# Feed-through matrices of a state space layer in four column groups of the array, their triangular form copied in sixteen pieces a chunk

## The chip, the cores and the metric

The kernel runs on one core of a Trainium2 chip. The metric is the device time of one execution in microseconds (us): the median of the runs is 2045.85 us (three runs, 2044.94 to 2045.88). Engines are named as the profile names them: PE (matrix products, its weight loads apart as PEld), DVE (vector), ACT (scalar), POOL and SP (DMA queue).

## The reference, cut to what matters

Two blocks run one after the other on 256 tokens of width 1024, all in float32: an attention and mixture-of-experts block, then a block with a retention layer, a gated feed-forward layer (ffn 0), a state space layer ("s5") and a second feed-forward layer (ffn 1). The change touches the set-up of the s5 layer alone. Of it the reference computes, for 64 groups of 16 inputs with 64 complex states each:

```python
mag = jnp.exp(lr * dt); ar = mag * jnp.cos(li * dt); ai = mag * jnp.sin(li * dt)
...
bbr = fr[..., None] * br - fi[..., None] * bi          # input matrix, real part; bbi likewise
...
_, _, s_r, s_i = lax.associative_scan(combine, (a_r, a_i, bu_r, bu_i), axis=0)
y = einsum('lbgp,gip->blgi', s_r, c_re) - einsum('lbgp,gip->blgi', s_i, c_im)
y = y.reshape(bsz, L, D_MODEL) + d_skip * u
```

The kernel doesn't scan over all 256 tokens. It takes four tokens as one step. Inside a step, output token n depends on input token m of the same step, for m no later than n, through a small matrix C A^(n-m) B, and for n = m through the skip weights `d_skip` too. Those matrices hold only weights, so they can be made at any time before the layer runs.

## The kernel before, in words

The 64 groups are worked off in eight chunks of eight groups. A chunk is four pairs q = 0 to 3, each of two groups, which is 32 inputs and 128 states. `s5_parts` makes one chunk's matrices and puts them into a scratch tensor in memory; the s5 layer loads them later. `second_block` calls it through `prepare`, at a priority lowered by LOW = 300, in the retention layer and the first 20 steps of ffn 0. The scheduler that builds the program then fits its instructions in between those of the layers: in the trace the products of the eight chunks run between 1405 and 1645 us, in the last product of the retention layer and in ffn 0. Each engine works through one fixed list in order, so an instruction that waits holds everything behind it.

For one chunk, `s5_parts` does this. POOL clears the buffers `R`, `o` and `T` (L1414 to L1416; each exists once, so it waits for the chunk before). DVE works out B times powers of A and C times powers of A (L1394, L1408). ACT copies them into `R` and `CA` (L1430, L1438, L1439). PE transposes `R` (L1443), ACT copies that (L1444), and a DMA on SP's queue stores it (L1445). Then the part that is changed: PE multiplies B with C A^n for the four pairs (L1449, eight products of 32 x 128 results, contraction over 128 states, real and imaginary part accumulated). All four pairs write to the same 32 rows of the bank, side by side. ACT copies the result to `K` (L1452, 32 partitions x 512). DVE adds the skip weights on the diagonal of token distance 0 (L1394 for `dd` and for `K`). ACT copies `K` four times into the block-triangular matrix `T`, block row st holding `K` shifted by 32 st columns (L1457, four copies of 32 partitions x 512, 384, 256 and 128). A DMA on SP's queue stores `T` (L1458). The priority is raised again (`high_priority`) for the copies and products.

Around it, the layers multiply streamed weights in three products each: every half panel of 128 x 1024 weights is split by ACT into a rounded part (L147) and by DVE into the rest (L148), and PE then makes 24 products with it (L251 to L253, 24 a half panel, 256 columns each). Splits run ahead of the products as far as buffers allow (`AHEAD` = 2, four buffers). ACT and DVE also do the activation of ffn 0 (L1602 to L1610).

Elsewhere the kernel already writes to column groups: `ada_tile` (L405), early in the program, multiplies 32 columns of weights into four of them, rows 32c to 32c+32 of one bank, 512 columns each.

Of the kernel before, what the change touches and what calls it, by code (L numbers as in the profile page):

```python
# [8 lines left out]
F32 = mybir.dt.float32  # L9
# [4 lines left out]
ALU = mybir.AluOpType  # L14
# [40 lines left out]
def bc(ap, dim, n):  # L55

    a = list(ap.ap)
    a.insert(dim, [0, n])
    return bass.AP(tensor=ap.tensor, offset=ap.offset, ap=a)
# [1317 lines left out]
def s5_parts(tc, g, c, tp, ps):  # L1377


    nc, A = tc.nc, g.A  # L1380
    v, s, pe = nc.vector, nc.scalar, nc.tensor
    q0 = 4 * c
    o = tp.tile([128, 2304], F32, tag="s5o", name="s5o")
    T = tp.tile([128, 4, 128], F32, tag="s5T", name="s5T")
    RT = o[:, 0:1024].rearrange("p (q i m) -> p q i m", q=4, i=2)
    CA = [o[:, 1024 + 640 * i:1664 + 640 * i].rearrange("p (q n) -> p q n", q=4) for i in range(2)]
    bcin = tp.tile([128, 4, 4, 16], F32, tag="s5b", name="s5b")
    nc.sync.dma_start(out=bcin, in_=A["s5_bc"][c])
    br, bi, cr, ci = (bcin[:, j] for j in range(4))
    fr, fi = (bc(g.fc[:, j, q0:q0 + 4], 2, 16) for j in range(2))  # L1390
    t = tp.tile([128, 4, 4, 16], F32, tag="s5t", name="s5t")

    def tt(o_, a, b, op):
        v.tensor_tensor(out=o_, in0=a, in1=b, op=op)  # L1394

    def powers(u, i0, n, x0, x1, ap, neg):

        ar, ai = (bc(ap[:, :, j, q0:q0 + 4], 3, 16) for j in range(2))
        y0, y1 = bc(x0, 1, n), bc(x1, 1, n)
        u0, u1 = (u[:, j, i0:i0 + n] for j in range(2))  # L1400
        tt(u0, ar, y0, ALU.mult)
        tt(t[:, :n], ai, y1, ALU.mult)
        tt(u0, u0, t[:, :n], ALU.subtract)
        tt(u1, ar, y1, ALU.mult)
        tt(t[:, :n], ai, y0, ALU.mult)
        if neg:
            u1, tn = (x.rearrange("p n q f -> p (n q f)") for x in (u1, t[:, :n]))
            v.scalar_tensor_tensor(out=u1, in0=u1, scalar=-1.0, in1=tn, op0=ALU.mult, op1=ALU.subtract)  # L1408
        else:
            tt(u1, u1, t[:, :n], ALU.add)  # L1410


    R = tp.tile([128, 2, 4, 4, 2, 16], F32, tag="s5R", name="s5R")
    nc.gpsimd.memset(R, 0.0)  # L1414
    nc.gpsimd.memset(o[:, 1024:2304], 0.0)
    nc.gpsimd.memset(T, 0.0)  # L1416
    u = tp.tile([128, 2, 4, 4, 16], F32, tag="s5u", name="s5u")
    b0, b1 = u[:, 0, 3], u[:, 1, 3]
    tt(b0, br, fr, ALU.mult)
    tt(t[:, 0], bi, fi, ALU.mult)  # L1420
    tt(b0, b0, t[:, 0], ALU.subtract)
    tt(b1, bi, fr, ALU.mult)
    tt(t[:, 0], br, fi, ALU.mult)
    tt(b1, b1, t[:, 0], ALU.add)
    powers(u, 0, 3, b0, b1, g.apr, False)
    with tc.high_priority():
        for j in range(2):
            for h in range(2):
                r = slice(64 * h, 64 * h + 64)
                s.copy(out=R[r, j, :, :, h].rearrange("p q s f -> p s q f"), in_=u[r, j])  # L1430
    u = tp.tile([128, 2, 4, 4, 16], F32, tag="s5u", name="s5u")
    powers(u, 0, 4, cr, ci, g.ap[:, 1:], True)
    with tc.high_priority():
        for j in range(2):
            for h in range(2):
                r = slice(64 * h, 64 * h + 64)
                ca = CA[j].rearrange("p q (n h f) -> p n q h f", n=5, h=2)[r, :, :, h]
                s.activation(out=ca[:, 0], in_=bcin[r, 2 + j], func=ACTF.Copy, scale=1.0 - 2.0 * j)  # L1438
                s.copy(out=ca[:, 1:], in_=u[r, j])  # L1439
        for j in range(2):  # L1440
            b = ps()
            for q in range(4):
                pe.transpose(out=b[:, q * 128:(q + 1) * 128], in_=R[:, j, q].rearrange("p s h f -> p (s h f)"), identity=g.ident)  # L1443
            s.copy(out=RT[:, :, j], in_=b.rearrange("p (q m) -> p q m", q=4))  # L1444
        nc.sync.dma_start(out=g.s5dram[c][:, :2304], in_=o)  # L1445
        b = ps()
        for q in range(4):
            for j in range(2):
                pe.matmul(out=b[:32, q * 128:(q + 1) * 128], lhsT=R[:, j, q, 3].rearrange("p h f -> p (h f)"), rhs=CA[j][:, q, :128],  # L1449
                          start=(j == 0), stop=(j == 1))  # L1450
        K = tp.tile([32, 4, 4, 32], F32, tag="s5K", name="s5K")
        s.copy(out=K, in_=b[:32].rearrange("p (q n m) -> p q n m", q=4, n=4))  # L1452
        dd = tp.tile([32, 4, 32], F32, tag="s5d", name="s5d")
        tt(dd, bc(g.ident[:32, :32], 1, 4), bc(g.s5d[:, q0:q0 + 4], 2, 32), ALU.mult)
        tt(K[:, :, 0], K[:, :, 0], dd, ALU.add)
        for st in range(4):
            s.copy(out=T[32 * st:32 * st + 32, :, 32 * st:128], in_=K[:, :, :4 - st].rearrange("p q n m -> p q (n m)"))  # L1457
        nc.sync.dma_start(out=g.s5dram[c][:, 2304:], in_=T.rearrange("p q n -> p (q n)"))  # L1458


def second_block(tc, g, out):
# [33 lines left out]
    def prepare(n=1):  # L1495

        for i in range(prepared[0], min(prepared[0] + n, 10)):
            with tc.high_priority(offset=-LOW):
                if i < 2:
                    s5_powers(tc, g, i, s5p)  # L1500
                else:
                    s5_parts(tc, g, i - 2, s5p, later_bank)
        prepared[0] += n
# [444 lines left out]
def tile_body(ctx, tc, A, out):  # L1948
    nc = tc.nc
    g = Ctx()  # L1950
    g.A, g.nc = A, nc
    cst = ctx.enter_context(tc.tile_pool(name="cst", bufs=1))
    wst = ctx.enter_context(tc.tile_pool(name="wstage", bufs=NSTAGE))
    wsp = ctx.enter_context(tc.tile_pool(name="wsplit", bufs=AHEAD + 2))
    st = Stream(nc, wst, NSTAGE, 2048)
# [72 lines left out]
    nc.vector.tensor_scalar(out=e, in0=e, scalar1=1.0, scalar2=None, op0=ALU.add)  # L2028
    nc.vector.reciprocal(out=e, in_=e)
    nc.vector.tensor_tensor(out=g.c2, in0=g.pv("c_2"), in1=e, op=ALU.mult)  # L2030
    g.s5d = cst.tile([32, 32], F32, name="s5d")
    nc.scalar.dma_start(out=g.s5d, in_=A["s5_d"])
    g.cst = cst
    g.ada = Columns(g, g.c2, mod2, g.pv("ada_b"), [ADA_ORDER.index(i) for i in (1, 4, 7, 10)])
# [16 lines left out]
def host_arrays(inputs):  # L2051
    import numpy as np

    def cat(*a):
        return np.ascontiguousarray(np.concatenate(a, axis=0))

    def colblocks(w, nb, kper):

        K, N = w.shape
        t = w.reshape(K // (128 * kper), kper, 128, N // nb, nb).transpose(3, 0, 2, 1, 4)  # L2060
        return t.reshape(-1, 128, kper * nb)
# [4 lines left out]
    I = {k: np.asarray(a) for k, a in inputs.items()}  # L2066
    d = {}
# [31 lines left out]
    bs = [I[f"s5_{n}_2"][0].reshape(8, 4, 2, 64, 16).transpose(0, 2, 3, 1, 4).reshape(8, 128, 4, 16) for n in ("b_re", "b_im")]  # L2099
    cs = [I[f"s5_{n}_2"][0].reshape(8, 4, 2, 16, 64).transpose(0, 2, 4, 1, 3).reshape(8, 128, 4, 16) for n in ("c_re", "c_im")]  # L2100
    d["s5_bc"] = np.stack(bs + cs, axis=2)
    d["s5_d"] = I["s5_d_2"][0].reshape(32, 32).T
    d["ada_w"] = cat(*(colblocks(I["ada_w_2"][i // 6][:, i % 6 * 1024:(i % 6 + 1) * 1024], *((512, 4) if i in ADA_PE else (1024, 2)))
                       for i in ADA_ORDER))

    def blocks(w, order):

        K, N = w.shape
        t = w.reshape(K // 128, 128, N // 128, 128).transpose(2, 0, 1, 3)[order]
# [14 lines left out]
    f = np.float32  # L2124
# [9 lines left out]
    c, s = np.cos(ang).astype(f), np.sin(ang).astype(f)  # L2134
# [28 lines left out]
```

## Time and profile before

| | |
|---|---|
| median of three runs | 2045.85 us |
| profiled execution | 2045.55 us |
| its span (first to last instruction) | 2043.9 us |
| mean granted clock of PE | 0.98 |
| PE busy | 1943.4 us, 95% |
| DVE busy | 1104.8 us, 54% |
| ACT busy | 649.2 us, 32% |

Shares over the whole span mix stages. From about 300 to 1200 us the expert layer streams weights; there DVE and ACT have little to do. In the retention layer and ffn 0 DVE is busy 80 to 95% and ACT 50 to 70% of the time. The difference between the profiled execution and its span, 1.65 us, lies before the first and behind the last instruction.

### The profile page before, as it was taken

The page shows a single profiled execution, that of the slowest core. Times are in us where ns is not written, and L with a number is a line of the kernel's source. Part 1 is how long each engine was busy: PE and PEld are TensorE (multiplying, and loading weights), DVE is VectorE, ACT ScalarE, POOL GpSimd, SP SyncE. Part 2 cuts the span into 40 slices and gives each one's busy share as a digit, 9 for nine tenths or more (in the row PEclk, how much of TensorE's full clock was granted, in tenths as well). Part 3 has the DMA queues.
Part 4 walks back from the last instruction along what each step waited for, and adds up shares of the span by engine and source line. Part 5 has one row for each costly group of instructions (what it writes and reads, how often), then busy time and mean ns, then how long its engine had stood idle before and what let it go on. Part 6 is the DMA issues. An engine that isn't in the chain of part 4 may idle for free. (4 is left out here: it accounts for less than half of the span.)

```text
span 2043.9 us, 29004 instructions
## 1 busy us (share of the span) xinstructions
PE 1943.4 (95%) x11188; PEld 1256.4 (61%) x11188; DVE 1104.8 (54%) x2360; ACT 649.2 (32%) x1134; POOL 59.0 (3%) x92
## 2 busy tenths in 40 slices
PE   6999989999999999999989999999999999999998
PEld 4756844333233333343333338888999998699998
DVE  3856654322222122132212238998898879779863
ACT  5455211000000000010000014445677645256542
POOL 1000010000000000000000000000011002100000
PEclk9999989999999999999999998999999999799999
DMA  8657659999999999999989994767677877555651
GB/s 342 223 197 282 240 193 413 427 426 427 426 427 427 426 427 427 426 421 387 427 366 427 426 394 159 259 235 267 228 258 260 288 279 295 206 193 195 226 178 63
DMA packets 101758, 643.41 MB, mean 315 GB/s; under 512 B 11584, under 2 KB 12880, under 8 KB 34288
## 3 DMA queue, kind: packets, MB, share of 16 engines
q1 hardware_dynamic: 94176, 613.46, 75.8%
q0 software_dynamic: 6624, 26.76, 3.8%
q8 instruction: 89, 1.46, 0.3%
q10 hardware_dynamic: 816, 1.30, 0.2%
q14 instruction: 53, 0.43, 0.1%
HBM read 626.79 MB, written 14.68 MB: 314 GB/s over the span
## 5 line engine op out<-in xcount | busy, mean ns | idle before, releaser
L956 PE MATMUL hc<-w,xe 128*64 128x512 f32 (+1 forms) x2008 | 470.3, 596 | 29.5 <-DMA w<-in_w_in_dram 28.3
L956 PEld LDWEIGHTS hc<-w,xe 128*64 128x64 f32 (+1 forms) x2008 | 145.4, 138 | 338.7 <-issue 244.0
L148 DVE TENSOR_TENSOR parts<-w,parts 128x1024 fp32r<-128x1024 f32 x238 | 289.8, 1222 | 64.2 <-ACT parts L147 60.0
L147 ACT CAST parts<-w 128x1024 fp32r<-128x1024 f32 x238 | 248.6, 1047 | 200.3 <-PE b L253 116.5
L251 PE MATMUL b<-h2h,parts 128*128 128x256 f32 x896 | 255.9, 286 | 1.4 <-ACT h2h L1527 0.9
L252 PE MATMUL b<-h2l,parts 128*128 128x256 f32 x896 | 255.5, 285 | 1.3 <-DVE h2l L1528 0.9
L956 PE MATMUL yb<-w,hb 128*64 128x512 f32 (+1 forms) x1024 | 252.5, 603 | 2.1 <-SPq L1205 1.6
L253 PE MATMUL b<-h2h,parts 128*128 128x256 f32 x896 | 254.3, 284 | 0.0
L976 DVE COPY hs<-hc 128x512 f32<-128x512 f32 x33 | 22.8, 691 | 405.3 <-PE hc L956 405.3
L251 PEld LDWEIGHTS b<-h2h,parts 128*128 128x128 f32 x896 | 170.1, 190 | 4.0 <-ACT h2h L1527 3.0
L252 PEld LDWEIGHTS b<-h2l,parts 128*128 128x128 f32 x896 | 169.9, 190 | 3.7 <-DVE h2l L1528 2.1
L253 PEld LDWEIGHTS b<-h2h,parts 128*128 128x128 f32 x896 | 169.8, 190 | 0.6 <-issue 0.6
L974 ACT COPY hs<-hc 128x512 f32<-128x512 f32 x33 | 19.3, 585 | 429.9 <-PE hc L956 429.9
L956 PEld LDWEIGHTS yb<-w,hb 128*64 128x64 f32 (+1 forms) x1024 | 68.1, 138 | 132.1 <-issue 120.9
L203 DVE SCALAR_TENSOR_TENSOR acc<-w,c,acc 128x1024 f32<-128x1024 f32 x77 | 98.5, 1279 | 7.3 <-DMA w<-in_ada_w_dram 7.0
L251 PE MATMUL b<-ah,parts 128*128 128x256 f32 x352 | 101.3, 288 | 0.7 <-ACT parts L147 0.6
L253 PE MATMUL b<-ah,parts 128*128 128x256 f32 x352 | 101.2, 287 | 0.0
L252 PE MATMUL b<-al,parts 128*128 128x256 f32 x352 | 100.5, 286 | 0.0
L938 PEld LDWEIGHTS gb<-S,h 128*128 128x128 f32 x544 | 68.2, 202 | 40.6 <-issue 30.9
L1019 ACT COPY ys<-yb 64x512 f32<-64x512 f32 (+1 forms) x32 | 18.5, 578 | 222.6 <-PE yb L956 222.5
L1562 PE MATMUL b<-parts,h2h 128*128 128x512 f32 x256 | 81.9, 400 | 1.4 <-DVE parts L148 0.8
L938 PE MATMUL gb<-S,h 128*128 128x128 f32 (+1 forms) x544 | 76.1, 293 | 6.2 <-issue 5.0
(521 smaller groups left out, 2967.0 us busy)
## 6 DMA issues: line engine op xcount, KB each, us to landing
w<-in_w_in_dram SPq DMA_DIRECT2D x252, 1024.0 KB, 19.4
w<-in_w_out_dram SPq DMA_DIRECT2D x128, 1024.0 KB, 19.5
w<-in_ffn_up_dram SPq DMA_DIRECT2D x44, 1024.0 KB, 4.9
w<-in_ada_w_dram SPq DMA_DIRECT2D x72, 512.0 KB, 5.1
w<-in_ret_w_in_dram SPq DMA_DIRECT2D x24, 1024.0 KB, 4.8
w<-in_ffn_down_dram SPq DMA_DIRECT2D x22, 1024.0 KB, 4.9
w<-in_w_ada_dram SPq DMA_DIRECT2D x32, 512.0 KB, 3.9
w<-in_ada_w_dram POOLq DMA_DIRECT2D x24, 512.0 KB, 4.8
```

The costliest lines, as they stand in the source:

```text
L147: self.nc.scalar.copy(out=hi, in_=w)
L148: self.nc.vector.tensor_tensor(out=lo, in0=w, in1=hi.bitcast(F32), op=ALU.subtract)
L203: v.scalar_tensor_tensor(out=self.acc, in0=w, scalar=cc, in1=self.acc, op0=ALU.mult, op1=ALU.add)
L251: pe.matmul(out=o, lhsT=w[0][:, sl], rhs=a[0][:, k], start=first, stop=False)
L252: pe.matmul(out=o, lhsT=w[0][:, sl], rhs=a[1][:, k], start=False, stop=False)
L253: pe.matmul(out=o, lhsT=w[1][:, sl], rhs=a[0][:, k], start=False, stop=last)
L938: g.got = pe.matmul(out=b[:, k * 128:k * 128 + n], lhsT=g.h2[:, t, d * 128:(d + 1) * 128], rhs=S[:, t, :n], start=(t == 0), stop=(t == 1))
L956: g.got = pe.matmul(out=on, lhsT=x, rhs=w[:, n * 512:n * 512 + 512], start=first, stop=last)
L974: s.copy(out=h, in_=hc[e][n])
L976: v.tensor_copy(out=h, in_=hc[e][n])
L1019: s.copy(out=o, in_=i)
L1562: pe.matmul(out=bs[t], lhsT=x[:, kk, tsl], rhs=y[:, k * 512:(k + 1) * 512], start=(kk == 0 and i == 0), stop=(kk == 7 and i == 2))
```

## The change

The eight products of a chunk go to four column groups: pair q writes rows 32q to 32q+32 of the bank, 128 columns, and the order is all four pairs with the real part, then all four with the imaginary part. `K` becomes 128 x 128. ACT copies only the 96 columns of token distances 1 to 3 out of the bank; the 32 columns of distance 0 are written by one DVE instruction that multiplies an identity by a per-partition skip weight and adds the bank. For this the skip weights come as 128 x 8 and not 32 x 32, and a tile `ident4` holds four 32 x 32 identities, made by four DVE copies at the start of the program. `T` is now set up with one copy for each pair and block row, as a pair's values lie on their own partitions: sixteen copies of 32 partitions, four each of 128, 96, 64 and 32 columns.

```diff
         nc.sync.dma_start(out=g.s5dram[c][:, :2304], in_=o)
+
         b = ps()
-        for q in range(4):
-            for j in range(2):
-                pe.matmul(out=b[:32, q * 128:(q + 1) * 128], lhsT=R[:, j, q, 3].rearrange("p h f -> p (h f)"), rhs=CA[j][:, q, :128],
+        for j in range(2):
+            for q in range(4):
+                pe.matmul(out=b[32 * q:32 * q + 32, :128], lhsT=R[:, j, q, 3].rearrange("p h f -> p (h f)"), rhs=CA[j][:, q, :128],
                           start=(j == 0), stop=(j == 1))
-        K = tp.tile([32, 4, 4, 32], F32, tag="s5K", name="s5K")
-        s.copy(out=K, in_=b[:32].rearrange("p (q n m) -> p q n m", q=4, n=4))
-        dd = tp.tile([32, 4, 32], F32, tag="s5d", name="s5d")
-        tt(dd, bc(g.ident[:32, :32], 1, 4), bc(g.s5d[:, q0:q0 + 4], 2, 32), ALU.mult)
-        tt(K[:, :, 0], K[:, :, 0], dd, ALU.add)
+        K = tp.tile([128, 128], F32, tag="s5K", name="s5K")
+        s.copy(out=K[:, 32:], in_=b[:, 32:128])
+        v.scalar_tensor_tensor(out=K[:, :32], in0=g.ident4, scalar=g.s5d[:, c:c + 1], in1=b[:, :32], op0=ALU.mult, op1=ALU.add)
         for st in range(4):
-            s.copy(out=T[32 * st:32 * st + 32, :, 32 * st:128], in_=K[:, :, :4 - st].rearrange("p q n m -> p q (n m)"))
+            for q in range(4):
+                s.copy(out=T[32 * st:32 * st + 32, q, 32 * st:128], in_=K[32 * q:32 * q + 32, :128 - 32 * st])
         nc.sync.dma_start(out=g.s5dram[c][:, 2304:], in_=T.rearrange("p q n -> p (q n)"))
...
-    g.s5d = cst.tile([32, 32], F32, name="s5d")
+    g.ident4 = cst.tile([128, 32], F32, name="ident4")
+    for q in range(4):
+        nc.vector.tensor_copy(out=g.ident4[32 * q:32 * q + 32], in_=g.ident[32 * q:32 * q + 32, 32 * q:32 * q + 32])
+    g.s5d = cst.tile([128, 8], F32, name="s5d")
     nc.scalar.dma_start(out=g.s5d, in_=A["s5_d"])
...
-    d["s5_d"] = I["s5_d_2"][0].reshape(32, 32).T
+    d["s5_d"] = I["s5_d_2"][0].reshape(8, 128).T
```

## Rows read from the trace of the kernel before

**Rows 1.** Page, part 1: busy time of each engine, share of span, instructions.
```profile
PE 1943.4 (95%) x11188; PEld 1256.4 (61%) x11188; DVE 1104.8 (54%) x2360; ACT 649.2 (32%) x1134; POOL 59.0 (3%) x92
```

**Rows 2.** Busy time by stretch; columns in the first line.
```profile
core 0: us, PE busy (x) PEld busy (x) DVE busy (x) ACT busy (x) POOL busy (x), PEclk, DMA share, GB/s
1400.00:1650.00 250.00, 243.97 (x1997) 235.96 (x1998) 213.77 (x407) 167.05 (x314) 18.37 (x21) 1.00 0.74 265
```

**Rows 3.** Line L1449: duration ns min/median/max, first and last start, form.
```profile
L1449 PE MATMUL x<-s5o,s5R x128: 269/273/297, 1405.6 to 1644.5; 128*32 128x128 f32 x128
```

**Rows 4.** Timeline, PE, chunk 0: start us, us, engine, line, tiles, count [idle before].
```profile
1405.19 0.28 PE L253 MATMUL b<-oh,parts 128*128 128x256 f32 x1
1405.64 1.91 PE L1449 MATMUL x<-s5o,s5R 128*32 128x128 f32 x16 [0.17 <-ACT s5o L1444]
1407.48 0.38 PE L251 MATMUL b<-oh,parts 128*128 128x256 f32 x1
```

**Rows 5.** Timeline, PE, of line L405: windows 31.80:31.83, 32.2:32.3 and 29:35 us.
```profile
31.80 0.64 PE L405 MATMUL pm<-w,cz 128*32 128x512 f32 x4
...
31.80 1.07 PE L405 MATMUL pm<-w,cz 128*32 128x512 f32 x8
...
31.80 2.78 PE L405 MATMUL pm<-w,cz 128*32 128x512 f32 x24
```

**Rows 6.** Groups by form, ACT, 1400 to 1650 us: line, count | busy us, mean ns.
```profile
L1457 ACT COPY s5T<-s5K 32x512 f32<-32x512 f32 x8 | 4.9, 617 | 2.2 <-DVE s5K L1394 2.1
L1452 ACT COPY s5K<-x 32x512 f32<-32x512 f32 x8 | 4.6, 577 | 8.4 <-PE x L1449 8.4
...
L1457 ACT COPY s5T<-s5K 32x384 f32<-32x384 f32 x8 | 4.1, 512 | 0.1
...
L1457 ACT COPY s5T<-s5K 32x256 f32<-32x256 f32 x8 | 3.2, 403 | 0.1
L1457 ACT COPY s5T<-s5K 32x128 f32<-32x128 f32 x8 | 2.4, 297 | 0.1
...
L316 ACT CAST eh<-mod 128x16 fp32r<-128x16 f32 x1 | 0.2, 208 | 0.0
```

**Rows 7.** Groups by form, DVE, 1400 to 1650 us.
```profile
L1394 DVE TENSOR_TENSOR s5K<-s5K,s5d 32x128 f32<-32x128 f32 x8 | 2.2, 275 | 3.3 <-ACT s5K L1452 3.3
L1394 DVE TENSOR_TENSOR s5d<-ident,s5d 32x128 f32<-32x128 f32 x7 | 1.9, 274 | 0.1
...
L216 DVE TENSOR_TENSOR mod<-x,pvt 128x8 f32<-128x8 f32 x4 | 0.6, 160 | 1.8 <-PE x L214 1.8
```

**Rows 8.** Waits of PE, 1400 to 1650 us: total us, times, longest.
```profile
PE x L1443 <- ACT s5o L1444: 0.8, 2, 0.7
...
PE x L1449 <- ACT s5o L1444: 0.6, 2, 0.4
PE b L251 <- ACT parts L147: 0.6, 1, 0.6
...
PE x L1443 <- ACT s5R L1430: 0.5, 2, 0.3
```

**Rows 9.** Waits of ACT, 1400 to 1650 us.
```profile
ACT parts L147 <- PE b L253: 24.9, 22, 2.8
...
ACT parts L147 <- DMA w<-in_ffn_up_dram: 0.7, 1, 0.7
```

**Rows 10.** Timeline, ACT, DVE and PE, from chunk 3's copies to the next split.
```profile
1523.55 1.24 ACT L1457 COPY s5T<-s5K 32x384 f32<-32x384 f32 x3
...
1525.96 1.05 ACT L147 CAST parts<-w 128x1024 fp32r<-128x1024 f32 x1
...
1527.07 1.22 DVE L148 TENSOR_TENSOR parts<-w,parts 128x1024 fp32r<-128x1024 f32 x1
...
1530.09 0.28 PE L251 MATMUL b<-h2h,parts 128*128 128x256 f32 x1
```

**Rows 11.** Timeline, ACT, DVE and PE, from chunk 0's copies to the next split.
```profile
1411.12 1.87 ACT L1457 COPY s5T<-s5K 32x512 f32<-32x512 f32 x4
...
1416.65 1.23 DVE L148 TENSOR_TENSOR parts<-w,parts 128x1024 fp32r<-128x1024 f32 x1 [2.32 <-ACT parts L147]
...
1420.37 0.36 PE L251 MATMUL b<-oh,parts 128*128 128x256 f32 x1
```

**Rows 12.** Waits of SP's queue, 1400 to 1650 us.
```profile
SPq L1458 <- ACT s5T L1457: 35.2, 8, 6.4
```

**Rows 13.** Timeline, DVE, first 16 us.
```profile
14.05 0.17 DVE L167 TENSOR_SCALAR rsx<-ss 128x4 f32<-128x4 f32 x1 [7.01 <-ACT xT L394]
```

## The prediction

> **What bounds the kernel now.** I read the page's engine line first: PE is busy 95% of the span, the others 54% and less [rows 1]. That is an average over unlike stages, so I then looked up where the changed lines run. The products of L1449 run from 1405.6 to 1644.5 us [rows 3], and the table by stretch for 1400 to 1650 us shows PE busy for 244.0 of 250 us, DVE for 213.8, ACT for 167.1, at a granted clock of 1.00, the 2.4 GHz level [rows 2]. The list of PE's waits in that stretch has no large entry: it waited 0.6 us for a split of weights, and 0.8, 0.6 and 0.5 us for the copies of the chunks themselves [rows 8]. ACT on the other hand waits 24.9 us for PE to give a buffer free before it may split on [rows 9]. So the reader is to see two things: here PE's own list of work sets the pace, so a microsecond taken out of it is a microsecond gained; and ACT has some 83 us of idle time, part of it because it runs ahead as far as buffers let it.
>
> **The change part by part.**
>
> The products (L1449). The records of the chip count two for each product: 128 for 64 products [rows 3], 16 a chunk. In chunk 0 the sixteen follow each other for 1.91 us; the last takes 0.27 us to its modelled end, so a step is (1.91 - 0.27) / 15 = 0.109 us [rows 3, 4]. PE's next product starts 1407.48 - 1405.64 = 1.84 us after the first one [rows 4]: fifteen steps and 0.20 us to change over. The change puts four neighbouring products on different column groups. The trace has this already, in L405: four records of 512 columns together take 0.64 us, eight 1.07 us, so every four cost 0.43 us, and twenty-four 2.78 us [rows 5]. One group alone would need 4 x 0.109 = 0.436 us for 512 columns of one record at L1449's rate. So four records cost there what one costs here: the groups run side by side, also in float32, and the two records of a product don't come in one another's way (the first four start together, then the second four). For a chunk after, this gives sixteen records in four steps: three steps of 0.109 and the same 0.20 us, 0.53 instead of 1.84 us. Saved: 1.31 us a chunk, 8 x 1.31 = 10.5 us. What L405 does not show are 128 columns and four different weight tiles, where a weight load has less time to hide. The bounds: if the two records of each product had to follow each other before the next group starts, sixteen records would need nine steps and 7 x 0.109 = 0.76 us a chunk would be saved, 6.1 us in all; if nothing overlaps, 0. I take 10.5, as the row of L405 is the same form of product in the same float32. The change into the 32-column form and out of it is paid before as well (0.45 us between L253 and L1449 where neighbours have 0.12 [rows 4]) and stays.
>
> The Trainium skill, "TensorE: Matmul & The Clock Gate", section "Measured speedup vs the span model", gives 3.07 times for four row groups and 2.38 times for three column groups, both less than the full factor. By 3.07, an estimate from that page, the sixteen steps of 1.74 us would shrink to 0.57 instead of 0.44 us and the saving to 1.17 us a chunk, 9.4 us in all. The row of L405 shows the full factor of four here, so I keep 10.5.
>
> ACT's copies. Before, a chunk takes 0.577 us for `K` and 0.617 + 0.512 + 0.403 + 0.297 = 1.83 us for `T` [rows 6]. The four sizes lie on a line of (617 - 297) / 384 = 0.83 ns a column on a base of 190 ns. By that, copies of 128, 96, 64 and 32 columns take 0.297, 0.270, 0.243 and 0.217 us, and four of each 4.11 us. The nearest rows bound one copy by 0.208 (128 x 16) and 0.297 us (32 x 128), so sixteen by 3.3 and 4.8 us. The copy of 96 columns out of the bank comes by the same line to 0.27 us, between 0.208 and 0.577. Sum: from 2.41 to 4.38 us, ACT +2.0 us a chunk, +15.8 us in all (bounds +1.1 to +2.9 a chunk). It lies beside PE's work: ACT is idle for 83 us of the stretch [rows 2]. But it comes as a burst in front of the next split, so the cover has to be looked at chunk by chunk. Every half panel feeds 24 products, so counted from the end each split can be put against its first product. Behind chunk 3's copies the split L147 starts at 1525.96, L148 ends at 1528.28, and PE begins on that half panel at 1530.09 and needs the second part 0.24 us later: 2.0 us of reserve [rows 10]. Behind chunk 0's the second part is ready at 1417.88 and wanted 0.32 us after 1420.37: 2.8 us [rows 11]. For the other six chunks I found 4.5 us or more in the same way. After the change splits come 2.0 us later and PE 1.3 us sooner, 3.3 us together: 1.3 us lost at chunk 3, 0.5 us at chunk 0, nothing elsewhere: 1.8 us.
>
> The waits of PE for the chunk's own copies (L1443, L1449) are 1.9 us now [rows 8]. Some of these copies stand behind another chunk's burst on ACT. Bounds 0 and 8 x 1.31 = 10.5 us (then the own chain takes all of the gain back); I take 1 us, near the first, since the row shows so little waiting now.
>
> DVE. The multiplication and the addition go, 0.274 + 0.275 us; one instruction of 128 x 32 comes, between 0.160 (128 x 8, read from a bank too) and 0.275 us (32 x 128) [rows 7], say 0.19. That is 0.36 us a chunk less, 2.9 us in all, on an engine that does not set the pace (214 of 250 us [rows 2]): nothing gained, 2.9 us at most. The addition had to wait for `K`; the new one waits for PE alone, beside ACT's copy. It holds the bank until DVE gets to it, but the next user of that bank is a transposition of the next chunk.
>
> SP's queue. The store of `T` waits in SP's list for the copies, 35.2 us over eight chunks [rows 12], with the loads of the streamed weights behind it. It will wait some 2 us longer each time. ACT waited for such weights only once, 0.7 us [rows 9]: the loads are more than 2 us ahead. Without that cover it would cost up to 2 us a chunk. POOL's next clearing of `T` waits for that store, and starts later by as much; it comes a chunk later.
>
> The start. Four DVE copies of 32 x 32 (0.16 to 0.28 us each [rows 7]) and a load of the same 4 KB: DVE is idle for 7.0 us before 14.05 us [rows 13], which hides them; 1 us if the cover were gone.
>
> The sum: -10.5 + 1.8 + 1 = -7.7 us. The profiled execution, 2045.55 us with its span of 2043.9 us, becomes 2037.9; the median of the runs stands 0.3 us above it, so 2038.1.
>
> **The rivals.**
>
> (a) The groups overlap by halves only, record after record: -6.1 + 1.8 + 0.5 = -3.8 us, 2042. Against it: the first four records of L405 run within 0.64 us [rows 5].
>
> (b) The chunk's own chain, or the new order in which the scheduler places everything behind the first chunk, eats the gain: PE reaches L1443 and L1449 sooner and waits there. For it: three of the four waits of [rows 8] are of this kind. Price 7 to 10 us of the gain: 2045 to 2048, no change.
>
> (c) Slower: ACT's burst holds up the splits. Place: the L147 behind each chunk's copies. It costs whatever 3.3 us exceed the reserve by, so it decides where the reserve falls under 3.3 us, and outweighs the products' gain only if PE loses more than 1.3 us a chunk. With no reserve at any chunk it would be 8 x 3.3 = 26 us against 10.5, 2061; with the reserve of chunk 3 at all of them 8 x 1.3 - 10.5, about 2046. So it needs reserves well under 2 us at most chunks, as a new order may bring; say 2 us lost more a chunk, 2054. Against it: two reserves of eight are under 3.3 us, and ACT is held back by buffers for 24.9 us. The Trainium skill, "TensorEngine Tiling (Array Packing)", section "PSUM Bottleneck", says that faster products in groups can leave the copy out of the bank as the bottleneck. In this trace ACT has a third of the stretch free, which speaks against it.
>
> (d) The products don't overlap at all, so the change does not do what it says: 0 + 1.8 gives 2047 to 2048. Against it: [rows 5].
>
> **How the numbers follow.** Forecast 0.61, its own range 2034 to 2042 (from -10.5 with 2 us of DVE's saving to the full 10.5 less 6); (a) 0.11; (b) 0.15; (c) 0.09; (d) 0.04. A measurement of this kernel can tell about 0.2%, 4.1 us, from no change: faster means under 2041.8, slower over 2049.9. Faster: 0.59 of the forecast and half of (a), 0.64. Slower: (c), 0.08. The rest, 0.28, is no change. The range for 8 in 10 takes in the forecast, (a) and most of (b) and goes to 2033 below for DVE's bound: 2033 to 2047.
>
> **What would show it.** Right: in the trace after, L1449 starts its sixteen records of a chunk in about 0.35 us, PE's next product follows 0.5 to 0.6 us after the first; L1457 has 128 copies of 0.21 to 0.30 us, 33 us in all; PE's waits for L147 and L148 in the stretch grow by some 2 us and the stretch shortens by about 8. Wrong: steps of L1449 that still follow each other; PE's waits at L1443, L1449, L251 that grow by 5 us or more; or a difference that arises outside 1400 to 1650 us, where nothing but the order can have changed.

## The result and the profile after

| | before | after |
|---|---|---|
| median of the runs made side by side | 2045.39 us (8 runs) | 2061.22 us (8 runs) |
| ratio | | 1.0072, interval 1.0053 to 1.0092 |
| profiled execution | 2045.55 us | 2057.06 us |
| its span | 2043.9 us | 2055.4 us |

The change makes the kernel slower, by 0.5 to 0.9%. The forecast was 2038.1 us with a range of 2033 to 2047; the time moved the other way, by 15.8 us in these runs. The way to the cause begins with a table by stage. It cuts both traces at the same products of PE: the first and last L956 for the expert layer, then the first product on the same half panels of the second block. Ahead of the experts lie 272.7 us in before and 272.6 in after. The "stretch" holds everything that the prediction worked on, and the s5 layer comes right behind it.

| us | experts | between | stretch | s5 layer | rest | tail |
|---|---|---|---|---|---|---|
| before | 947.3 | 175.9 | 297.7 | 94.4 | 242.6 | 13.2 |
| after | 957.7 | 174.8 | 291.3 | 103.9 | 241.3 | 13.7 |
| difference | +10.4 | -1.1 | **-6.4** | +9.5 | -1.3 | +0.5 |

The stretch is 6.4 us shorter, near the forecast of -7.7. But 2.0 us of that has only moved: eight products of L214 (two records each) and one of L301 (0.24 us) run at the end of the stretch in before and at the start of the s5 layer in after:

```profile
1675.30 1.92 PE L214 MATMUL x<-ones,acc 128*128 128x1 f32 x16
```
```profile
1704.05 1.84 PE L214 MATMUL x<-ones,acc 128*128 128x1 f32 x16
```

So the gain there is 4.4 us. Two stages whose instructions were not touched lost several times as much.

First the stretch. The lines that answer to [rows 3, 4] are, in after, the source view of the products (L1450 now: duration in ns min/median/max, first and last start, form) and the timeline of chunk 0:

```profile
L1450 PE MATMUL x<-s5o,s5R x128: 269/273/298, 1415.5 to 1649.7; 128*32 128x128 f32 x128
```
```profile
1415.53 0.64 PE L1450 MATMUL x<-s5o,s5R 128*32 128x128 f32 x16 [0.17 <-ACT s5o L1444]
1416.10 0.39 PE L251 MATMUL b<-oh,parts 128*128 128x256 f32 x1
```

Each record still takes 273 ns, but sixteen now fit in 0.64 us instead of 1.91, and PE's next product starts 0.57 us after the first. ACT's and DVE's groups by form in the stretch (busy us, mean ns of one), against [rows 6, 7]:

```profile
L1457 ACT COPY s5T<-s5K 32x128 f32<-32x128 f32 x32 | 9.5, 297 | 2.2 <-DVE s5K L1454 1.4 <-issue 0.5
L1457 ACT COPY s5T<-s5K 32x96 f32<-32x96 f32 x32 | 8.7, 270 | 0.4
L1457 ACT COPY s5T<-s5K 32x64 f32<-32x64 f32 x30 | 7.3, 242 | 0.3
L1457 ACT COPY s5T<-s5K 32x32 f32<-32x32 f32 x28 | 6.0, 215 | 0.3
L1453 ACT COPY s5K<-x 128x96 f32<-128x96 f32 x8 | 1.9, 239 | 2.7 <-PE x L1450 2.4
L1454 DVE SCALAR_TENSOR_TENSOR s5K<-ident,s5d,x 128x32 f32<-128x32 f32 x8 | 2.0, 247 | 1.5 <-ACT s5K L1453 1.5
```

PE's largest waits in the stretch (total us, times, longest), against [rows 8], and SP's, against [rows 12]:

```profile
PE b L251 <- DVE eo L339: 2.0, 1, 2.0
PE b L253 <- DVE parts L148: 1.7, 2, 1.0
PE x L1443 <- issue: 1.3, 1, 1.3
PE x L1443 <- ACT s5R L1430: 1.2, 2, 1.0
PE x L1443 <- POOL s5o L1415: 0.9, 1, 0.9
PE x L1443 <- ACT s5o L1444: 0.8, 3, 0.3
...
PE x L1450 <- ACT s5o L1444: 0.5, 2, 0.3
...
PE b L251 <- ACT parts L147: 0.3, 1, 0.3
```
```profile
SPq L1458 <- ACT s5T L1457: 45.8, 8, 6.5
```

All waits listed for PE in the whole stretch of the table sum to 11.0 us, against 5.1 before.

Then the expert layer, from 273 to 1230 us. Busy time by stretch for 500 to 1100 us (us and records of PE, PEld, DVE, ACT, POOL; then granted clock, DMA share, GB/s) and the DMA issues of its weights (KB each, median us to landing), both of before and then both of after:

```profile
500.00:1100.00 600.00, 567.35 (x2518) 212.37 (x2516) 146.76 (x293) 47.39 (x84) 0.00 (x0) 0.99 1.00 417
```
```profile
w<-in_w_in_dram SPq DMA_DIRECT2D x158, 1024.0 KB, 19.5
```
```profile
500.00:1100.00 600.00, 560.66 (x2476) 209.71 (x2478) 145.38 (x291) 46.78 (x83) 0.00 (x0) 0.99 1.00 413
```
```profile
w<-in_w_in_dram SPq DMA_DIRECT2D x158, 1024.0 KB, 19.8
```

The DMA share is 1.00 in both: this layer is bound by its stream of weights. In the same 600 us the stream brings less, 413 against 417 GB/s (in most slices of the page 420 against 427), and every engine has done less by the end. So the transfers themselves are slower. What differs for them is where they land: `ident4` (128 bytes a partition) and the new `s5d` (32) take 160 bytes where the old `s5d` took 128. In the built program everything allocated behind them from that end of the memory lies 32 bytes further; the weights' staging buffers begin 34080 bytes into a partition instead of at 34048, a multiple of 256.

Last the s5 layer. Its instructions are unchanged, but for the 2.0 us that moved in; their order and the clock are not. Busy time in pieces of the layer, first before, then after (columns as above; the seventh number behind the window's length is the granted clock):

```profile
1718.00:1726.00 8.00, 7.42 (x58) 6.28 (x57) 7.88 (x19) 5.91 (x10) 2.38 (x4) 1.00 0.75 304
1726.00:1736.00 10.00, 9.35 (x82) 9.15 (x81) 9.35 (x20) 1.63 (x3) 3.05 (x5) 0.98 0.89 323
1736.00:1746.00 10.00, 10.00 (x36) 6.72 (x35) 7.17 (x14) 0.80 (x2) 2.75 (x5) 0.50 0.78 285
1746.00:1754.00 8.00, 8.00 (x59) 6.26 (x59) 5.16 (x13) 4.24 (x7) 1.85 (x4) 1.00 0.76 263
```
```profile
1720.00:1728.00 8.00, 7.21 (x64) 7.10 (x63) 7.87 (x17) 6.44 (x11) 1.80 (x3) 1.00 0.96 365
1728.00:1738.00 10.00, 10.00 (x53) 10.00 (x51) 8.69 (x18) 1.71 (x4) 2.31 (x4) 0.53 0.69 230
1738.00:1748.00 10.00, 10.00 (x49) 10.00 (x48) 1.93 (x5) 1.23 (x2) 1.24 (x2) 0.50 0.24 74
1748.00:1756.00 8.00, 8.00 (x30) 5.66 (x29) 8.00 (x18) 0.40 (x1) 2.19 (x4) 0.50 0.39 139
```

In before the clock lies at 0.50, the 1.2 GHz level, for some 10 us; in after for some 27. PE is busy all that time, at half speed. Summed over the layer, (1 - clock) times its length gives 11.9 us lost before and 22.2 after: 10.3 us, and the layer is 9.5 longer. What PE did ahead of the fall stands in its timeline (start us, us, line, count [idle before <- releaser]), first before, then after:

```profile
1718.87 1.97 PE L1790 MATMUL b<-U,s5i 128*128 128x64 f32 x16 [0.20 <-DMA s5i<-s_scratch]
1720.77 1.02 PE L229 MATMUL s<-w,c 128*1 128x512 f32 x2
1721.72 0.66 PE L1827 MATMUL c<-S,s5i 128*128 128x64 f32 x4
```
```profile
1723.81 1.95 PE L1790 MATMUL b<-U,s5i 128*128 128x64 f32 x16
1725.60 0.39 PE L1825 MATMUL c<-U,s5i 128*128 128x64 f32 x2
1726.77 0.67 PE L1827 MATMUL c<-S,s5i 128*128 128x64 f32 x4 [0.79 <-DVE S L1813]
...
1728.62 0.57 PE L1825 MATMUL c<-U,s5i 128*128 128x64 f32 x2
```

Before, a product of L229 (two records, 1.0 us of a modulation column for a later layer) fills the time until DVE's scan has written `S`. After, the scheduler has put that product ahead of the first block of L1790, PE waits 0.79 us, and 1.9 us later its products have become half as fast (0.57 us for the two records of a product of L1825 instead of 0.39).

There are two suspects, then: the addresses, and an order or a clock that may be chance. The runs are to tell them apart from each other and from the rival that the change's own work costs the time.

### The profile page after: what moved, and what is told of

Its sections match the earlier page's. It is cut to its first block, busy times and chain, and to the rows that moved or that the text cites. A ratio compares the mean times of both kernels' runs of the same rounds, so it can differ in the third digit from the quotient of the medians.

```text
span 2055.4 us, 29105 instructions
## 1 busy us (share of the span) xinstructions
PE 1940.9 (94%) x11188; PEld 1253.7 (61%) x11188; DVE 1102.7 (54%) x2356; ACT 662.6 (32%) x1230; POOL 58.8 (3%) x92
## 5 line engine op out<-in xcount | busy, mean ns | idle before, releaser
L956 PE MATMUL hc<-w,xe 128*64 128x512 f32 (+1 forms) x2008 | 471.4, 597 | 37.5 <-DMA w<-in_w_in_dram 36.2
L956 PEld LDWEIGHTS hc<-w,xe 128*64 128x64 f32 (+1 forms) x2008 | 144.5, 138 | 348.7 <-issue 238.6
L956 PE MATMUL yb<-w,hb 128*64 128x512 f32 (+1 forms) x1024 | 252.7, 603 | 2.2 <-SPq L1205 1.6
L253 PE MATMUL b<-h2h,parts 128*128 128x256 f32 x896 | 254.6, 285 | 0.0
L253 PEld LDWEIGHTS b<-h2h,parts 128*128 128x128 f32 x896 | 170.5, 190 | 0.2 <-issue 0.2
L956 PEld LDWEIGHTS yb<-w,hb 128*64 128x64 f32 (+1 forms) x1024 | 68.1, 138 | 132.3 <-issue 120.2
L253 PE MATMUL b<-ah,parts 128*128 128x256 f32 x352 | 100.6, 286 | 0.0
```

Source lines behind the costliest of these rows:

```text
L253: pe.matmul(out=o, lhsT=w[1][:, sl], rhs=a[0][:, k], start=False, stop=last)
L956: g.got = pe.matmul(out=on, lhsT=x, rhs=w[:, n * 512:n * 512 + 512], start=first, stop=last)
```

## The experiments

For every run the mean granted clock of each execution is known, and over all of them the time goes with it: one line a kernel with a common slope fits 193 executions to 2.1 us, and the slope is 1.73 us for each thousandth of the clock. So two numbers stand beside each median: the mean clock of its executions, and the time at one common clock, 0.978, by that fit (± is 95%).

| kernel | median us (runs) | ratio to before, interval | mean clock | us at clock 0.978 | profiled: experts, stretch, s5 layer |
|---|---|---|---|---|---|
| before | 2047.7 (84) | | 0.9792 ± 0.0005 | 2050.3 ± 0.4 | 947.3, 297.7, 94.4 |
| after | 2061.2 (8) | 1.0072 (1.0053 to 1.0092) | 0.9757 ± 0.0018 | 2057.9 ± 1.4 | 957.7, 291.3, 103.9 |
| b_pad32 | 2059.8 (9) | 1.0062 (1.0038 to 1.0086) | 0.9790 ± 0.0016 | 2062.7 ± 1.3 | 956.8, 300.9, 94.0 |
| b_pad128 | 2062.2 (10) | 1.0055 (1.0031 to 1.0080) | 0.9779 ± 0.0018 | 2061.4 ± 1.3 | 959.7, 300.5, 95.7 |
| a_pad224 | 2051.6 (12) | 1.0010 (0.9991 to 1.0030) | 0.9755 ± 0.0016 | 2046.3 ± 1.2 | 950.2, 294.0, 104.0 |
| b_16copies | 2045.7 (12) | 0.9999 (0.9979 to 1.0019) | 0.9793 ± 0.0015 | 2049.9 ± 1.2 | 949.3, 299.4, 91.1 |
| a_pad224_4copies | 2051.4 (12) | 1.0017 (1.0000 to 1.0035) | 0.9743 ± 0.0014 | 2044.0 ± 1.2 | 945.7, 290.3, 94.5 |
| a_pad224_order | 2051.7 (12) | 1.0011 (0.9987 to 1.0035) | 0.9757 ± 0.0023 | 2046.5 ± 1.2 | 946.7, 292.8, 92.3 |
| a_pad224_swap | 2054.9 (12) | 1.0028 (1.0005 to 1.0051) | 0.9739 ± 0.0011 | 2047.7 ± 1.2 | 950.2, 294.6, 100.9 |
| a_pad224_pool | 2079.4 (4) | 1.0151 (1.0107 to 1.0194) | 0.969 | not fitted | 946.0, 316.4, 101.0 |
| **a_pad224_fill** | **2042.5 (11)** | **0.9981 (0.9965 to 0.9998)** | 0.9792 ± 0.0017 | 2046.2 ± 1.2 | 949.6, 294.6, 94.2 |
| b_early | 2051.4 (12) | 1.0026 (1.0012 to 1.0040) | 0.9776 ± 0.0009 | 2051.1 ± 1.2 | 946.3, 301.6, 96.8 |

Each ratio is to runs of before made beside that kernel; the first row is over all of these but the eight beside after. The stages are those of one execution each. The ratio and the two columns on the clock leave out one execution of a_pad224, 2070.9 us at a clock of 0.964. How far one execution can be trusted for a stage, the stretch shows: b_early has PE's order of before in it, and takes 301.6 us where before took 297.7.

**The address alone.** The kernel before, with an unused constant of 32 bytes a partition:

```diff
     nc.scalar.dma_start(out=g.s5d, in_=A["s5_d"])
+    pad = cst.tile([128, 8], F32, name="pad")
+    nc.vector.memset(pad, 0.0)
```

> The kernel before, with 32 bytes a partition added to the constants at the place where the change adds its 32, so that every buffer behind them, the weight buffers first, starts 32 bytes later; the work and its order are the same (one small DVE memset more). Theory A, address: the expert layer, which the change doesn't touch and which lost 10 us, slows down because the weight buffers no longer start at a multiple of 256 bytes. Then this kernel loses some 10 us in the expert layer and ends at 2053 to 2058 us, and its median transfer spacing there rises from 2.45 to 2.49 us. Theory B, the change's own instructions or program do it: this kernel stays at 2045 us. Whether the s5 layer, which lost 9 us, slows here too tells whether that loss is of the address or of the new order.

The expert layer takes 956.8 us, as in after, and the same view shows the same stream:

```profile
500.00:1100.00 600.00, 561.16 (x2485) 208.75 (x2482) 145.35 (x291) 46.76 (x83) 0.00 (x0) 1.00 1.00 413
```

Mean clock and s5 layer are those of before. So 32 bytes of nothing cost 12.4 us at equal clock. With 128 bytes (`[128, 32]`):

> The kernel before with a constant tile of 128 bytes a partition more, so that everything behind it lies 128 bytes further, as 32 bytes did in b_pad32 (expert layer 956.8 us against 947.3). If a target address that is a multiple of 256 bytes is what the stream of weights needs, the expert layer takes 953 us or more and the run comes out 4 us or more above the kernel before; how much, next to b_pad32, tells whether the loss goes with the size of the shift. If a multiple of 64 or 128 bytes is enough, the expert layer takes 947 to 950 us and the run is within 3 us of the kernel before. If the new placement of whole buffers against each other did it (and not the last bits of the address), the loss could be of any size.

959.7 us and 413 GB/s again, 11.1 us at equal clock. Shifts of 32 and 128 bytes cost alike, so it is not a matter of the size of the shift. A shift of 128 is not harmless; one of 256 is, as the next run shows.

**The change with the addresses put right.** After, with a constant of 224 bytes (`[128, 56]`), so that all that follows lies 256 bytes behind its place in before:

> The changed kernel with 224 bytes a partition more of constants, so that the buffers behind them move by 256 bytes in all against the kernel before and stand as before in steps of 256; its order is that of the changed kernel. Theory A: the expert layer gets its 10 us back; with the gain of the products, 2038 to 2048 us, depending on whether the s5 layer's 9 us belong to the address too (then about 2040) or to the order (then about 2049). Theory B: it stays at 2055 to 2061 us.

The expert layer is back to 950.2 us and, at equal clock, the kernel is 11.6 us faster than after and 4.0 us faster than before. Its median isn't faster than before's: the s5 layer still takes 104.0 us, and the mean clock is as low as in after.

Which buffers it is can be read from the traces and the addresses of the built programs. The stream goes round eleven landing buffers. Eight of them move with the constants (four of the staging pool, four of the pool for splits) and start at multiples of 256 bytes in before. Three are allocated from the other end of the memory, don't move, and start 96 bytes past such a multiple in both kernels. From one landing to the next, from 330 to 1150 us, the medians for the two groups of four and for the three are:

| us for 1 MB | staging | splits | the three that stay |
|---|---|---|---|
| before | 2.451 | 2.430 | 2.479 |
| a_pad224 | 2.449 | 2.432 | 2.480 |
| after | 2.493 | 2.492 | 2.485 |
| b_pad32 | 2.492 | 2.491 | 2.487 |
| b_pad128 | 2.485 | 2.486 | 2.483 |

So the slow transfers are those into buffers that don't start at a multiple of 256 bytes, in one and the same execution of before too.

**The copies alone.** The kernel before with `T` set up in sixteen copies:

```diff
-            s.copy(out=T[32 * st:32 * st + 32, :, 32 * st:128], in_=K[:, :, :4 - st].rearrange("p q n m -> p q (n m)"))
+            for q in range(4):
+                s.copy(out=T[32 * st:32 * st + 32, q, 32 * st:128], in_=K[:, q, :4 - st].rearrange("p n m -> p (n m)"))
```

> The kernel before with the triangular matrix set up in sixteen copies a chunk instead of four; products, addresses and everything else as before. This is the ACT part of the change alone. The prediction's account (copies hidden but for 1.8 us, and up to some us more): 2046 to 2050 us. Rival, the burst of copies holds up the splits at most chunks: 8 times 2 us, 2060 us or more.

No change that can be told: 0.9999, at equal clock -0.4 ± 1.3 us. The stretch of its one profiled execution is 1.7 us longer, although L214's eight products have moved out of it here too; that is within what one execution can show. With the old products, then, ACT's burst does not cost PE a time that can be told, and it does not lower the clock.

**The groups with few copies.** a_pad224 with four copies of the old sizes; they write pair 0's values for all four pairs, so the other pairs' matrices are left out:

```diff
-            for q in range(4):
-                s.copy(out=T[32 * st:32 * st + 32, q, 32 * st:128], in_=K[32 * q:32 * q + 32, :128 - 32 * st])
+            s.copy(out=T[32 * st:32 * st + 32, :, 32 * st:128], in_=bc(K[:32, :128 - 32 * st], 1, 4))
```

> The changed kernel with the 224 bytes of a_pad224, and the triangular matrix set up in four copies a chunk of the old sizes, with pair 0's values for all four pairs: the other pairs' values are left out, so that the products in column groups stand alone without the sixteen copies. The prediction's account: 10 us under the kernel before if the address is set right, 2035 to 2040 us, and 2 to 4 us under a_pad224. Rival, the copies cost much: 10 us or more under a_pad224.

At equal clock it is 2.3 ± 1.7 us faster than a_pad224; the stretch is 290.3 us, with 8.0 us of waits listed for PE instead of 12.3. That is what the burst costs with the new products. The mean clock is low here too, so it isn't the copies that lower it. Its profiled execution, 2037.8 us, was the fastest of its twelve, so that one execution says little here.

**The order, first try.** Two kernels were to give TensorE's program in the s5 layer its old order, one by dependencies on L1790, one by exchanging two lines:

```diff
-                rotated_inputs(c + 1)
+                rotated_inputs(c + 1, {2: lambda: last_of[0].ins, 3: lambda: first_of[1], 4: lambda: last_of[1].ins, 5: lambda: first_of[2]}.get(c, lambda: None)())
```

> The change with all later buffers at the addresses of before plus 256 bytes, and with four dependencies that hold TensorE's products of L1790 back, so that TensorE's program in the state space layer has the order that it had before the change (in a_pad224 twenty-four products of L1790, three blocks, stand in a row). If that order caused the 9 to 10 us that the state space layer lost in the two looks at it (103.9 and 104.0 us against 94.4, 94.0 and 91.1), the layer takes 91 to 96 us, the changed stretch 291 to 294, and the run comes out at 2040 to 2043, 4 to 7 us below the kernel before. If the loss is the chance of TensorE's clock in those executions, the layer can take anything between 91 and 104 us, and the median stays at that of a_pad224, about 2051.

```diff
-        s.copy(out=K[:, 32:], in_=b[:, 32:128])
         v.scalar_tensor_tensor(out=K[:, :32], in0=g.ident4, scalar=g.s5d[:, c:c + 1], in1=b[:, :32], op0=ALU.mult, op1=ALU.add)
+        s.copy(out=K[:, 32:], in_=b[:, 32:128])
```

> The change at the same addresses as a_pad224, with the DVE instruction on the diagonal written ahead of ACT's copy out of the bank: nothing but these two lines. The scheduler then places TensorE's products in the state space layer in the order of before of itself. By the theory of the order: as a_pad224_order, state space layer 91 to 96 us, 2040 to 2043. By chance of the clock: layer between 91 and 104, median about 2051. If the prediction's step on the products holds, the changed stretch is 291 to 294 us in either case.

Neither edit did what its expectation says of it. In the traces a_pad224_swap has TensorE's order of after, and a_pad224_order has parted only the three blocks of L1790; in both the product of L229 still stands ahead of the first block of L1790, and PE waits 0.78 us for `S`. The medians and mean clocks are those of a_pad224. So the three blocks in a row are not the cause. a_pad224_order shows how much is left to chance: its executions spread from 2037.6 to 2059.9 us, with mean clocks of 0.982 to 0.970, and in the profiled one the same 0.78 us of waiting was followed by some 27 us more at a clock of 1.00.

**POOL for the copies.** a_pad224 with `nc.gpsimd.tensor_copy` for the sixteen copies:

> The change at the same addresses as a_pad224, with the sixteen copies of T on POOL instead of ACT. TensorE's order in the state space layer stays as in a_pad224 (three blocks of L1790 in a row). By the theory of the order: state space layer about 104 us and the run about 2050 whatever the copies do. By chance of the clock: layer between 91 and 104. If ACT's burst cost 2 us in the changed stretch, as predicted, the stretch is about 290 us against 294.0 of a_pad224; if POOL's slower copies then keep the store of T and the next chunk's clearing waiting, it is no shorter.

Worse than either theory allowed: the stretch takes 316.4 us and PE waits 27.9 us in it (before 5.1). ACT is the better place for these copies.

**The filler put back.** a_pad224 with one dependency: the second of the two products of L229's second part is held behind the third block of L1790, near its place in before.

```diff
-                ada.part(small_bank, p5)
+                hold = at[0] == 1
+                ada.part(small_bank, p5, (lambda odd: tc.issue_after(rotated[2]) if odd else nullcontext()) if hold else None)
```

> The change at the addresses of a_pad224, with one dependency: the fourth pair of products of L229 (1.0 us of TensorE's work) is held behind the third block of L1790, where TensorE's program of before has it. In after, a_pad224, a_pad224_order and a_pad224_swap that pair stands earlier, and TensorE waits 0.78 to 0.79 us for DVE's scan (S, L1813) in its place; in the kernels of before's kind it waits for no scan there. Theory of the gap: this wait lets TensorE's clock fall more often. Then it is gone here, the mean granted clock over the runs is 0.978 to 0.980 (a_pad224 0.975, a_pad224_order 0.976, a_pad224_swap 0.974; before 0.979), the state space layer takes 90 to 96 us, and the median is 2043 to 2046, some 4 us below the kernel before (at equal clock 0.978 the change is 4 us ahead: 2044.5 against 2048.7 us of span). Rival, that another part of the change or of the order lowers the clock: mean clock 0.974 to 0.976, median 2050 to 2055. Chance: no such difference between the kernels would repeat at all.

PE's timeline there (this kernel's lines are numbered one higher):

```profile
1721.12 1.95 PE L1791 MATMUL b<-U,s5i 128*128 128x64 f32 x16
1723.00 1.02 PE L230 MATMUL s<-w,c 128*1 128x512 f32 x2
1724.24 0.41 PE L1828 MATMUL c<-S,s5i 128*128 128x64 f32 x2 [0.22 <-DVE S L1814]
```

The wait is down to 0.22 us, the mean clock is 0.9792, as in before, the s5 layer takes 94.2 us, and the median is 2042.5: 0.19% below the kernel before (interval 0.02 to 0.35%), and the lowest median of this study. At equal clock it stands with a_pad224 (2046.2 and 2046.3), so the difference between the two goes with the clock. The dependency isn't the only difference in the program: the scheduler moved some products of L1790, L1825 and L1827 in the layer along with it.

**The reverse.** The kernel before, its addresses and set-up untouched, with the priority of that part raised, so that its last product comes early:

```diff
-                ada.part(small_bank, p5)
+                with tc.high_priority(offset=(150 if at[0] == 1 else 0)):
+                    ada.part(small_bank, p5)
```

> The reverse: the kernel before, its addresses and its set-up of the matrices unchanged, with the priority of the second of L229's parts raised by 150, so that its last pair of products comes ahead of the second block of L1790 and TensorE goes from that block straight to the products that need DVE's scan. Theory of the gap: TensorE waits 0.8 us or more for S there, the mean granted clock over the runs falls from 0.979 to about 0.975, and the median rises by some 7 us (1.8 us a thousandth of the clock, over all runs so far) to 2054 to 2058. Rival, that the change's own parts lower the clock: mean clock stays at 0.978 to 0.980, median 2045 to 2050.

Half of what was expected: clock 0.9776, not 0.975, and 2051.4 us, 3.7 above before instead of 7. PE's timeline shows a wait of 1.15 us, at another place (35 us into the layer, not 30), as the scheduler moved other products too, and from there on half speed:

```profile
1734.44 1.09 PE L1827 MATMUL c<-S,s5i 128*128 128x64 f32 x4 [1.15 <-DVE S L1813]
```

The direction is confirmed without any of the change's own parts, its size is not: how long the clock stays down differs between orders, and why is open.

The profiled executions also show where the clock is lost. Outside the s5 layer (1 - clock) times the length comes to 27 to 33 us in all of them but a_pad224_pool, whichever order they have. In the layer it is 7 to 14 us in the five with L229's product in its place (before, b_pad32, b_pad128, b_16copies, a_pad224_fill), 15.4 in b_early, and 22.2, 22.2, 18.8, 10.2 and 6.8 in after, a_pad224, a_pad224_swap, a_pad224_4copies and a_pad224_order. In the first five the layer's first fall comes behind a wait too, but later (39 to 47 us into the layer, not 32) and lasts 3 to 14 us.

## Why the prediction was wrong

**The sum of after.** Against before over all runs (2047.7 us; the eight beside after had 2045.4) after's 2061.2 is +13.5 us. The address costs +11.6 us (after against a_pad224 at equal clock), the lower clock (0.9792 - 0.9757) x 1.73 us a thousandth = +6.1 us, the change's own work -4.0 us (a_pad224 against before at equal clock). Together +13.7. That the three meet the total proves nothing, as the fit splits it so; what ties each to its cause are the runs: b_pad32 and b_pad128 for the first, a_pad224_fill and in part b_early for the second.

**The products: right.** The steps foretold 0.53 us from the first product to PE's next, and -10.5 us in all. Measured: 0.57 where the sixteen stay together, as in three chunks, and twice 0.36 us in the five where the scheduler parts them eight and eight. Over eight chunks that is 5.3 us instead of 15.2: -9.9 us. The row of L405 was the right guide, and rivals (a) and (d) are out. The factor of 3.07 for row groups that was weighed from the Trainium skill's "TensorE: Matmul & The Clock Gate", "Measured speedup vs the span model", would have given 0.57 for the sixteen steps alone, or 0.53 for the fifteen from the first start to the last. Here these take 0.37 us (0.57 less 0.20 to change over) and took 1.64, so the trace goes with four full column groups.

**ACT and DVE: right in their rows, somewhat low in their effect.** The four sizes came to 297, 270, 242 and 215 ns (foretold 297, 270, 243, 217), the copy of 96 columns to 239 (270), DVE's instruction to 247 (190). That this instruction would wait for PE alone was wrong: its row names ACT's copy of `K` (L1453) behind 1.5 us of waiting. The store of `T` waits 45.8 - 35.2 = 10.6 us longer on SP's queue, 1.3 a chunk (foretold some 2). The burst's price was put at 1.8 us; a_pad224_4copies says 2.3 ± 1.7.

**PE's own waits: mis-sized.** All added waits were put at 1.8 + 1 = 2.8 us. They are 11.0 - 5.1 = 5.9 us in after and 7.2 in a_pad224, most of it at L1443 behind copies and clearings of the chunk, and at the end of the retention layer (L339). This is the mild form of rival (b): it took 3 to 4 us more of the gain than the sum allowed. In after -9.9 and +5.9 make -4.0, and the stretch shows -6.4, of which 2.0 only moved into the s5 layer: -4.4. The whole kernel at equal clock gives the same, 4.0 us for a_pad224 against before, not 7.7. Rival (c) did not come: `T`'s copies held up the splits by 2 us at L253, not by the 1.3 us a chunk, 10.5 in all, that it needed.

**The start: the step that failed.** It costed the new constants by DVE's idle time and their load, which is right: four copies of 170 ns vanish in it.

```profile
L2033 DVE COPY ident<-ident 32x32 f32<-32x32 f32 x4 | 0.7, 170 | 0.0
```

But it asked only what the new tiles take in time, not what they take in memory. 32 bytes more in a list of constants moved eight of the eleven buffers that the weights land in, and the stage bound by their stream lost 10 us. No row of the profile of before shows that price, though its landings hold it (2.48 against 2.43 and 2.45 us a megabyte). It did show a DMA share of 1.00 from 500 to 1100 us, so whatever touches the stream's buffers had to be looked at. The Trainium skill, "DMA: Bandwidth & Descriptors", section "How a descriptor splits into AXI transactions", says that when a descriptor doesn't start at a multiple of 256 bytes its first transaction starts at the multiple below, and the bytes ahead of the start still cost beats; it says so of what is read. Here it is the written side that moved, 32 and 128 bytes both cost, 256 don't, and the measured loss is 1.0 to 1.3% of the layer (9.5 to 12.4 of 947 us). Direction and the multiple of 256 agree; that this splitting is the mechanism isn't shown.

**Outside the stretch.** The prediction named "a difference that arises outside 1400 to 1650 us, where nothing but the order can have changed" as a sign against it, and put no price on it. The order did change: with the changed set-up the scheduler moved a filler of 1.0 us in another stage, and the lower clock of the kernels with that order is worth 6 us. Rival (b) had the new order in mind, but only inside the stretch.

**Open.** It is open why PE's clock stays down for 27 us in after, a_pad224 and a_pad224_swap while PE is busy all the time, and for about 10 us in before; and whether the wait itself or another part of that order makes the fall likelier, since no run moved the wait alone. Not tried either is to align the three landing buffers that before itself has 96 bytes off: by its landings, 0.04 us for each of some 105 megabytes, that would be worth about 4 us, an estimate.

## What to carry to other kernels

When an edit adds or resizes a tile, write down the byte offset of every buffer allocated behind it, first of all of those that a bandwidth-bound stream lands in; keep them at multiples of 256 bytes and try an unused pad of the right size before blaming the edit. When a stage has changed its length, look first whether work has moved across its border. Where the scheduler places work by itself, compare each engine's order in all later stages, and look for short fillers that no longer cover a wait. Where the mean granted clock differs from execution to execution, compare kernels at equal clock too: it parts what an edit does from what the clock does with it.

## What the runs showed of the hardware

- Eight of eleven landing buffers that begin 32 or 128 bytes past a multiple of 256 made a stream at a DMA share of 1.00 bring 420 instead of 427 GB/s; the next megabyte landed after 2.49 us instead of 2.43 to 2.45. In the kernel before, three buffers that begin 96 bytes past one took 2.48 us beside the others' 2.43 to 2.45.
- A single wait of PE of 0.79 us, in work that otherwise keeps it busy, was followed 1.9 us later by a granted clock of 0.50 for some 27 us, PE busy throughout. The same wait of 0.78 us left the clock at 1.00 for some 27 us in another execution. The kernels with the order that has a wait there, of 0.78 to 0.95 us (after, a_pad224, a_pad224_order, a_pad224_swap, a_pad224_4copies) have mean clocks of 0.974 to 0.976, a_pad224_fill, with 0.22 us left of it, has 0.979; the difference is worth 6 to 9 us.
- Four products of 32 columns in four column groups ran side by side in float32 also with four different weight tiles and only 128 columns: sixteen records start within 0.37 us, and each still takes 273 ns.
